# S5 channels copied unscaled from PSUM, the 1/rms applied on transposed chunks, with a new step order and a mirrored table

## The chip, the cores and the metric

The kernel runs on one core of one Trainium2 chip, in one launch. The metric is the device time of that launch in microseconds (us). TensorE (PE) multiplies matrices, VectorE (DVE) and ScalarE (ACT) work on elements, GpSimd (POOL) does so too and issues one of the two big DMA queues, SyncE (SP) issues the other. Each engine runs its own list of instructions in order and waits on semaphores for the others.

## The reference, cut to what matters

A two-layer encoder works on 512 prompt tokens and 32 sample tokens. Layer A, in which everything of this change lies:

```python
z = rms_norm(h, norm_mix_g[layer]) @ w_mix_in[layer]      # 1024 -> 768 S5 channels + 256 memory channels
mq = rms_norm(z_mem per head, mem_q_norm_g[layer])
mem_out = memory_attend(mq, mem_k[layer], mem_v[layer])   # 4 heads, 256 memory tokens
# S5: 48 groups of 16 channels, 64 complex states each
bu = einsum(z_mix per group, bb);  h_t = lam * h_{t-1} + bu_t;  y = Re(c h) + d_skip * u
y = gelu(y);  mix_out = y * sigmoid(y @ w_glu + b_glu)
h = h + concatenate([mix_out, mem_out]) @ w_mix_out[layer]
h = h + conv_ffn(rms_norm(h, norm_ffn_g[layer]))
```

Layer B has latent attention in place of S5. The rms_norm is x * rsqrt(mean(x²) + eps) * g. The gain g lies in the weights' side of the product, and 1/rms is one number for each token, so it can be multiplied on after the product with w_mix_in.

## The kernel before, in words

Activations lie with channels on the partitions and the 544 tokens along the free axis. Every big fp32 weight block is loaded raw by SP (`wraw`), rounded by ACT to a high half (`whi`, L231), reduced by ACT to what is left with its sign turned (`wlo`, L232), and completed by an accumulating DMA of POOL (L233). Three buffers of each kind are in use. A product is then three matmuls for each block and each of two column halves of 272 (`gemm`, L324). The order of instructions is worked out while the kernel is built: code that stands later is moved ahead by the priorities of the table `ORDER` (L63), which `pri` and `unit` apply, and buffers come from first-in first-out lists (`Slots`).

The input product gives eight tiles of 128 channels: six for S5 (`zts`), two for the memory attention (`zm`). `z0_end` (L963 to L976) takes each from PSUM with three (or two) DVE multiplications by `rb`, a tile in which 1/rms of every token is broadcast to all partitions (`norm_bcast`). Tokens are grouped into 69 chunks of 8 (64 of the prompt, one of zeros, 4 of the sample).

S5 is worked as six steps, one for each tile of 8 groups.
- `s5_params` (L544 to L668) builds once, on DVE, the table `tab` of the powers of lambda over chunks by doubling (levels of L646 to L649), and the powers inside a chunk `prd`.
- `s5_wv` and `s5_wvt` make the matrices that map a chunk's input to its end state. `s5_wc` (L693 to L715) makes those that map the state to the 8 outputs (three DVE operations, L698 and L700), and with matmuls (L704) the kernel taps inside a chunk; the taps `kp` are completed on POOL (L711), written to DRAM (`kd`, L714) and read back as Toeplitz blocks by 8 POOL loads (`s5_kernel`, L717 to L725).
- `s5_input` (L727 to L747) transposes a tile so that chunks lie on the 69 partitions (L733), ACT copies it out of PSUM (L735), and transposes it back in another order (L743, L744).
- `s5_scan` (L749 to L787): two matmul groups, then DVE: multiply by the table (L767 on), a running sum (L774), multiply back (L777), combine (L783, L784). It ends with `hh`, the states.
- `s5_output` (L789 to L812): L795 multiplies inputs by the Toeplitz blocks, L796 the states by `wc`, ACT copies (L800), transposes (L807), GELU (L808, L809).

The step loop (L1047 to L1073) writes, for step m: scan m, input m+1, output m-1, and at the end `do_wc(m+1)`. `mem_kv` (L335 to L406, matmuls L347, transposes L401), the keys and values of the prompt's memory tokens, is put between as a filler. After the loop come output 5, and the GLU loop (L1088 to L1099, six products by `w_glu` with L324). `mem_attend` (L417 to L523) is a generator: one piece (the norms: L427 to L452) and the first part stand ahead of the GLU loop, the others inside it at m = 1, 2, 4 and 5. `mix_out` (L814) follows.

Of the kernel before, what the change touches and what calls it, by code (L numbers as in the profile page):

```python
# [20 lines left out]
NS = 32  # L21
# [29 lines left out]
for _n, _w in (("mix", 2 * KD), ("bglu", NM), ("ffn", 2 * KD), ("kv", KD), ("mem", 2 * KD), ("ql", NM),  # L51
# [12 lines left out]
         "s5_input": 260, "norm0": 20, "s5_params": -50, "mem_attend0": 100, "s5_wc": 10, "q_front0": 10, "norm1": 0,  # L64
# [73 lines left out]
def body(ctx, tc, A, O):  # L138
# [5 lines left out]
    FW = 576  # L144
# [39 lines left out]
    warm = F.get(576)  # L184
# [3 lines left out]
    for _ in range(2):  # L188
        T.matmul(b, warm[:, 64:192], warm[:, 64:], start=True, stop=True)
# [90 lines left out]
    def norm_bcast(r, bs):  # L280
# [5 lines left out]
        rb = F.get(NT)  # L286
        V.tensor_copy(rb[:, :NP], pa)
        V.tensor_copy(rb[:, S0:], pb[:, :NS])
        bs.put(pa, pb)
        return rb  # L290
# [126 lines left out]
    def mem_attend(l, zm, kv_p, kv_s, fm, bm, out):  # L417
        ktp, vp = kv_p
        kts, vs = kv_s
# [21 lines left out]
        r = rsqrt(x, 128, 17, "zr")  # L441
        mx, nm, su, ri = (sm(17, n) for n in ("zmx", "znm", "zsu", "zri"))
# [101 lines left out]
    def s5_params(pool, tmp, sp5):  # L544
# [93 lines left out]
        V.memset(tab[:, 0, :, 0:1], 1.0)  # L638
        V.memset(tab[:, 1, :, 0:1], 0.0)
        SR = NPR * 70  # L640
        for o, lvl, c0, n in ((1, 0, 0, 1), (2, 1, 0, 2), (4, 2, 0, 4), (8, 3, 0, 8), (16, 4, 0, 16), (32, 5, 0, 16),
                              (48, 5, 16, 16), (64, 6, 0, 1)):
            t0 = view(tmp, [[NPR * n, 2], [n, NPR], [1, n]])
            t1 = view(tmp, [[NPR * n, 2], [n, NPR], [1, n]], H)
            src = view(tab, [[SR, 2], [70, NPR], [1, n]], c0)
            V.tensor_tensor(t0, src, view(sc, [[0, 2], [1, NPR], [0, n]], NPR * (lvl + 1)), ALU.mult)  # L646
            V.tensor_tensor(t1, src, view(sc, [[0, 2], [1, NPR], [0, n]], NPR * (8 + lvl + 1)), ALU.mult)
            V.tensor_tensor(tab[:, 0, :, o:o + n], t0[:, 0], t1[:, 1], ALU.subtract)
            V.tensor_tensor(tab[:, 1, :, o:o + n], t0[:, 1], t1[:, 0], ALU.add)  # L649
        V.tensor_copy(view(tab, [[70, 2 * NPR], [1, 5]], 65), view(tab, [[70, 2 * NPR], [1, 5]]))  # L650

        prd = pool.tile([128, 2, 9, 48], F32, name="prd")
        xq = pool.tile([128, 49, 16], F32, name="xq")
        P.memset(xq[:, 48], 0.0)
        for half in range(2):
            a = slice(64 * half, 64 * half + 64)
            for gh in range(2):
                c = slice(64 * gh, 64 * gh + 64)
                for i, src in enumerate((pr, pi)):
                    S.activation(view(prd[a], [[48, 9], [8, NM], [1, 4]], 432 * i + 4 * gh),  # L660
                                 view(src[c], [[NPR, 9], [4, NM], [1, 4]]), AF.Copy)
# [4 lines left out]
        P.memset(q["kp"], 0.0)  # L666
        q["hf"] = pool.tile([128, NM, 8, 2], F32, name="hf")
# [25 lines left out]
    def s5_wc(q, m, fs, fd, fb, bs):  # L693

        pk = bs.get(512)
        c, d = fd.get(8, 9, 16), fb.get(8, 9, 16)
        for o, x in ((c, 0), (d, 1)):
            V.tensor_tensor(o, view(q["cc"], [[16, 8], [0, 9], [1, 16]], 16 * (48 * x + 8 * m)),  # L698
                            view(q["prd"], [[1, 8], [48, 9], [0, 16]], 432 * x + 8 * m), ALU.mult)
# [27 lines left out]
    def s5_input(zt, fs, bs):  # L727

        zT = [fs.get(4, 8, 16, p=69) for _ in range(2)]
        for qd in range(2):  # L730
            b = bs.get(512)
            for s_ in range(4):
                T.transpose(b[:69, 128 * s_:128 * s_ + 128], view(zt, [[8, 69]], 7 - 4 * qd - s_), ident)  # L733
            for gh in range(2):
                S.activation(view(zT[gh], [[128, 4], [16, 4], [1, 16]], 64 * qd),  # L735
                             view(b[:69], [[16, 4], [128, 4], [1, 16]], 64 * gh), AF.Copy)
            bs.put(b)
        yield
        u = fs.get(8, 69)
        for gh in range(2):  # L740
            b = bs.get(512)
            for i in range(4):
                T.transpose(b[:, 69 * i:69 * i + 69], zT[gh][:, i].rearrange("p a b -> p (a b)"), ident[:69, :69])  # L743
            S.activation(u[:, 4 * gh:4 * gh + 4, :].rearrange("p a b -> p (a b)"), b[:, :276], AF.Copy)  # L744
            bs.put(b)
        fs.put(*zT)
# [42 lines left out]
    def s5_output(u, wc, kk, hh, yg, fs, bs):  # L789
        yT = [fs.get(4, 8, 16, p=69) for _ in range(2)]  # L790
        b = [bs.get(512) for _ in range(2)]
        for gh in range(2):
            for i in range(4):
                o = b[gh][:69, 128 * i:128 * i + 128]
                T.matmul(o, u[:, 4 * gh + i, :], kk[gh][:, i], start=True, stop=False)  # L795
                T.matmul(o, hh[:, 4 * gh + i, 0:69], wc[:, 4 * gh + i, 1:9].rearrange("p a b -> p (a b)"), start=False,  # L796
# [167 lines left out]
    def z0_end(m, ps, bs):  # L964
        if m < NM:
            zt = FY.get(552)
            P.memset(zt[:, 512:520], 0.0)
            V.tensor_tensor(zt[:, 0:272], ps[0][:, :272], rb[:, :272], ALU.mult)
            V.tensor_tensor(zt[:, 272:512], ps[1][:, :240], rb[:, 272:512], ALU.mult)
            V.tensor_tensor(zt[:, 520:552], ps[1][:, 240:272], rb[:, S0:], ALU.mult)  # L970
            zts.append(zt)
        else:
            z = F.get(NT)
            evac_rows(z, ps, rb)
# [18 lines left out]
    with pri("norm0"):  # L993
        rb = norm_bcast(r0, BS)
# [29 lines left out]
    wvs = []  # L1024
# [11 lines left out]
    g_in, g_out = s5_input(zts[0], F, BS), None  # L1036
# [8 lines left out]
    for m in range(NM):  # L1045
# [18 lines left out]
        if m < NM - 1:  # L1064
            do_wc(m + 1)
# [19 lines left out]
    mo = []  # L1085
# [719 lines left out]
```

## Time and profile before

| | before |
|---|---|
| median of 3 runs | 1437.56 us (1436.07 to 1439.15) |
| the profiled run | 1436.17 us |
| its span | 1434.4 us |
| busy: PE, DVE, ACT, POOL | 98%, 50%, 52%, 27% |
| last scan's last DVE operation begins | 150.33 us |
| first GLU matmul | 171.45 us |

The profile shows one execution. "Busy" is the time in which an engine has an instruction in work; matmuls are pipelined, so a busy PE is not a PE at its peak. A window is a stretch of the span. PEclk is the granted clock of TensorE as a share of its full speed. The chain of waits goes back from the last instruction, at each step to what released it. Times of instructions overlap by a little on one engine, so the spacing from one start to the next says better what one costs.

### The profile page before, as it was taken

The page shows a single profiled execution, that of the slowest core. Times are in us where ns is not written, and L with a number is a line of the kernel's source. Part 1 is how long each engine was busy: PE and PEld are TensorE (multiplying, and loading weights), DVE is VectorE, ACT ScalarE, POOL GpSimd, SP SyncE. Part 2 cuts the span into 40 slices and gives each one's busy share as a digit, 9 for nine tenths or more (in the row PEclk, how much of TensorE's full clock was granted, in tenths as well). Part 3 has the DMA queues.
Part 4 walks back from the last instruction along what each step waited for, and adds up shares of the span by engine and source line. Part 5 has one row for each costly group of instructions (what it writes and reads, how often), then busy time and mean ns, then how long its engine had stood idle before and what let it go on. Part 6 is the DMA issues. An engine that isn't in the chain of part 4 may idle for free.

```text
span 1434.4 us, 26764 instructions
## 1 busy us (share of the span) xinstructions
PE 1402.3 (98%) x10661; PEld 1299.2 (91%) x10661; DVE 714.6 (50%) x1776; ACT 740.6 (52%) x1237; POOL 385.7 (27%) x668
## 2 busy tenths in 40 slices
PE   7999899999999999999989999999999999999998
PEld 6966689999999999999978986558999999999998
DVE  7999642555315541555357545663455514551351
ACT  6556464655435543555644554654565534553452
POOL 2065333222111211133336222332322211221121
PEclk8999899999999999999999999999999999999999
DMA  9443548788788888868741521103778887888775
GB/s 268 109 118 104 151 109 190 161 173 180 171 175 175 175 175 175 176 145 196 154 118 56 158 71 45 30 1 74 170 169 176 176 177 173 176 175 177 171 157 140
DMA packets 66045, 210.59 MB, mean 147 GB/s; under 512 B 9152, under 2 KB 11424, under 8 KB 65920
## 3 DMA queue, kind: packets, MB, share of 16 engines
q0 software_dynamic: 29152, 96.61, 37.4%
q1 hardware_dynamic: 35616, 110.17, 26.6%
q10 hardware_dynamic: 1152, 2.10, 0.4%
q8 instruction: 84, 1.38, 0.4%
q14 instruction: 41, 0.34, 0.1%
HBM read 203.22 MB, written 5.61 MB: 146 GB/s over the span
## 4 chain that ended last, share of the span: by engine, by line
PE 87%; DMA 4%; DVE 3%; ACT 2%; issue 2%; POOL 1%; SPq 0%; ACTq 0%; DVEq 0%; POOLq 0%
PE bank L324 67%; PE bank L1312 2%; PE bank L1560 2%; PE bank L1399 2%; PE bank L1596 1%; DMA wlo<-i_w_in 1%; PE bank L1513 1%; PE bank L1487 1%; PE bank L1585 1%; PE bank L347 1%; DMA wlo<-i_w_f 1%; PE bank L1201 1%; PE bank L479 1%; PE bank L1427 1%; PE bank L517 1%
## 5 line engine op out<-in xcount | busy, mean ns | idle before, releaser
L324 PE MATMUL bank<-rc,whi 128*128 128x272 f32 x3728 | 625.3, 289 | 0.2 <-DVE rc L305 0.2
L324 PEld LDWEIGHTS bank<-rc,whi 128*128 128x128 f32 x3728 | 528.2, 188 | 4.2 <-issue 3.1
L324 PE MATMUL bank<-rc,wlo 128*128 128x272 f32 x1864 | 388.3, 288 | 0.5 <-DMA wlo<-i_w_in 0.3
L231 ACT ACTIVATE whi<-wraw 128x1024 fp32r<-128x1024 f32 (+2 forms) x178 | 182.9, 1028 | 354.3 <-issue 304.0
L324 PEld LDWEIGHTS bank<-rc,wlo 128*128 128x128 f32 x1864 | 293.2, 188 | 1.3 <-DMA wlo<-i_w_in 0.5
L324 PE MATMUL bank<-g,whi 128*128 128x272 f32 x1408 | 234.8, 288 | 0.8 <-ACT g L216 0.8
L324 PEld LDWEIGHTS bank<-g,whi 128*128 128x128 f32 x1408 | 198.9, 188 | 1.4 <-ACT g L216 1.2
L233 POOL DMA_DIRECT2D wlo<-i_w_f x136 | 116.7, 858 | 303.9 <-ACT wlo L232 302.5
L232 ACT ACTIVATE wlo<-wraw 128x1024 fp32r<-128x1024 f32 (+2 forms) x178 | 180.6, 1015 | 0.6 <-PE bank L1513 0.5
L324 PE MATMUL bank<-g,wlo 128*128 128x272 f32 x704 | 145.6, 288 | 2.1 <-DMA wlo<-i_w_f 2.1
L855 DVE SCALAR_TENSOR_TENSOR fa<-fa,gp,fa 128x546 f32<-128x546 f32 x88 | 69.6, 791 | 139.6 <-ACT fa L854 139.6
L869 DVE TENSOR_TENSOR h<-bank,h 128x272 f32<-128x272 f32 x96 | 38.2, 435 | 173.2 <-PE bank L324 172.6
L324 PEld LDWEIGHTS bank<-g,wlo 128*128 128x128 f32 x704 | 110.3, 188 | 2.5 <-DMA wlo<-i_w_f 2.5
L854 ACT ACTIVATE fa<-fa,gp 128x546 f32<-128x546 f32 x88 | 73.1, 831 | 12.5 <-DVE fa L849 12.5
L847 DVE TENSOR_TENSOR fa<-bank,fa 128x272 f32<-128x272 f32 x88 | 38.9, 442 | 80.5 <-PE bank L324 76.7
L856 DVE SCALAR_TENSOR_TENSOR fa<-fa,gp,fa 128x546 f32<-128x546 f32 x88 | 69.5, 790 | 3.1
L895 ACT ACTIVATE fa<-fa 128x546 f32<-128x546 f32 x44 | 29.1, 662 | 71.7 <-DVE fa L856 71.7
L851 POOL COPY fa<-gp 128x2 f32<-128x2 f32 x88 | 19.9, 227 | 170.2 <-DVE g L217 107.9
L852 POOL COPY fa<-fa 128x4 f32<-128x4 f32 x88 | 18.2, 207 | 164.5 <-DVE fa L849 164.5
L324 PE MATMUL bank<-ra,whi 128*128 128x272 f32 x256 | 47.7, 309 | 2.7 <-ACT whi L241 2.7
L216 ACT ACTIVATE g<-fa 128x544 fp32r<-128x544 f32 x44 | 28.9, 658 | 37.6 <-DVE fa L897 37.6
L896 DVE TENSOR_TENSOR fa<-fa,fa 128x512 f32<-128x512 f32 x44 | 30.5, 693 | 33.5 <-ACT fa L895 33.5
(628 smaller groups left out, 1987.2 us busy)
## 6 DMA issues: line engine op xcount, KB each, us to landing
wraw<-i_w_f SPq DMA_DIRECT2D x120, 512.0 KB, 4.9
wlo<-i_w_f POOLq DMA_DIRECT2D x120, 512.0 KB, 7.4
wraw<-i_w_out SPq DMA_DIRECT2D x16, 512.0 KB, 4.4
wlo<-i_w_out POOLq DMA_DIRECT2D x16, 512.0 KB, 7.0
wraw<-i_w_in SPq DMA_DIRECT2D x14, 512.0 KB, 5.1
wlo<-i_w_in POOLq DMA_DIRECT2D x14, 512.0 KB, 7.5
wraw<-i_w_f SPq DMA_DIRECT2D x16, 384.0 KB, 3.1
wlo<-i_w_f POOLq DMA_DIRECT2D x16, 384.0 KB, 5.9
```

The costliest lines, as they stand in the source:

```text
L216: S.activation(hi, src, AF.Copy)
L231: S.activation(hi, raw, AF.Copy)
L232: S.activation(lo, raw, AF.Copy, scale=-1.0)
L233: P.dma_start(lo, ap, accum_op=ALU.add)
L324: T.matmul(ps[q][:, :c], ww, xx[:, c0:c0 + c], start=k == 0 and i == 0, stop=k == n - 1 and i == 2)
L847: V.tensor_tensor(u[:, 2:274], ps[0][:, :272], rb[:, :272], ALU.mult)
L854: S.activation(y, u[:, 2:548], AF.Identity, scale=gcol("cw", 3 * ci + 2), bias=gcol("cb", ci))
L855: V.scalar_tensor_tensor(y, u[:, 1:547], gcol("cw", 3 * ci + 1), y, ALU.mult, ALU.add)
L856: V.scalar_tensor_tensor(y, u[:, 0:546], gcol("cw", 3 * ci), y, ALU.mult, ALU.add)
L869: V.tensor_tensor(h[m][:, c0:c0 + cc], ps[qd][:, :cc], h[m][:, c0:c0 + cc], ALU.add)
L895: S.activation(yg, yg, AF.Silu)
L896: V.tensor_tensor(u[:, 2:514], ya[:, :NP], yg[:, :NP], ALU.mult)
```

## The change

The S5 stage is changed in four ways.

First, the six S5 tiles are copied from PSUM by ACT without 1/rms. `rb` gets a gap of 8 zeros between prompt and sample so that it has the same 69 chunks of 8, and 8 PE transposes and 2 ACT copies make from it `sr`, 69 chunks by 8 positions. In `s5_input`, where chunks are on the partitions, ACT's copies multiply by a column of `sr`; there are 8 copies of 128 elements per partition and step in place of 4 of 256. The copies go to one tile (`FZ`, a part of the memory in which the table's scratch lay).

Second, the table is centred: column 32 holds power 0, and columns 0 to 31 are the mirror of columns 33 to 64 with the imaginary part's sign turned, copied by ACT. Two levels of the doubling go.

Third, the powers inside a chunk go from 9 to 8, `wc` from 1152 to 1024 elements, the matmul of the taps is split into 16 and 112 columns, and the D-skip term is made once.

Fourth, the order: `do_wc(m+1)` stands ahead of input m+1, not at the end of step m; the norms of the memory attention are a unit at m = 3, and its other pieces stand at m = 1 to 5 of the GLU loop, with a new priority. A few buffer counts and widths follow.

```diff
-         "s5_input": 260, "norm0": 20, "s5_params": -50, "mem_attend0": 100, "s5_wc": 10, "q_front0": 10, "norm1": 0,
+         "s5_input": 260, "norm0": 20, "s5_params": -50, "mem_attend0": 30, "s5_wc": 10, "q_front0": 10, "norm1": 0,
...
-        for o, lvl, c0, n in ((1, 0, 0, 1), (2, 1, 0, 2), (4, 2, 0, 4), (8, 3, 0, 8), (16, 4, 0, 16), (32, 5, 0, 16),
-                              (48, 5, 16, 16), (64, 6, 0, 1)):
+        for o, lvl, c0, n in ((1, 0, 0, 1), (2, 1, 0, 2), (4, 2, 0, 4), (8, 3, 0, 8), (16, 4, 0, 16), (32, 5, 0, 1)):
...
-        V.tensor_copy(view(tab, [[70, 2 * NPR], [1, 5]], 65), view(tab, [[70, 2 * NPR], [1, 5]]))
+        for i, s in ((0, 1.0), (1, -1.0)):
+            S.activation(tab[:, i, :, 0:32], view(tab, [[70, NPR], [-1, 32]], SR * i + 64), AF.Copy, scale=s)
+        S.activation(view(tab, [[70, 2 * NPR], [1, 5]], 65), view(tab, [[70, 2 * NPR], [1, 5]], 32), AF.Copy)
...
-        c, d = fd.get(8, 9, 16), fb.get(8, 9, 16)
+        c, d = fd.get(8, 8, 16), fb.get(8, 8, 16)
...
-                T.matmul(pk[32 * i:32 * i + 32, 128 * gh:128 * gh + 128],
-                         view(q["xq"], [[1, 32]], 16 * (8 * m + 4 * gh + i)),
-                         c[:, 4 * gh + i, 0:8].rearrange("p a b -> p (a b)"), start=True, stop=True)
+                T.matmul(o[:, :16], x, q["cc"][:, 0, 8 * m + g], start=True, stop=True)
+                T.matmul(o[:, 16:], x, c[:, g, 0:7].rearrange("p a b -> p (a b)"), start=True, stop=True)
...
-            for gh in range(2):
-                S.activation(view(zT[gh], [[128, 4], [16, 4], [1, 16]], 64 * qd),
-                             view(b[:69], [[16, 4], [128, 4], [1, 16]], 64 * gh), AF.Copy)
+            for s_ in range(4):
+                s = 7 - 4 * qd - s_
+                S.activation(view(zT, [[128, 8], [1, 16]], 64 * qd + 16 * s_), view(b[:69], [[16, 8], [1, 16]], 128 * s_),
+                             AF.Copy, scale=sr[:, s:s + 1])
...
-            V.tensor_tensor(zt[:, 0:272], ps[0][:, :272], rb[:, :272], ALU.mult)
-            V.tensor_tensor(zt[:, 272:512], ps[1][:, :240], rb[:, 272:512], ALU.mult)
-            V.tensor_tensor(zt[:, 520:552], ps[1][:, 240:272], rb[:, S0:], ALU.mult)
+            S.activation(zt[:, 0:272], ps[0][:, :272], AF.Copy)
+            S.activation(zt[:, 272:512], ps[1][:, :240], AF.Copy)
+            S.activation(zt[:, 520:552], ps[1][:, 240:272], AF.Copy)
...
+        for qd in range(2):
+            b = BS.get(512)
+            for s_ in range(4):
+                T.transpose(b[:69, 128 * s_:128 * s_ + 128], view(rb, [[8, 69]], 4 * qd + s_), ident)
+            S.activation(sr[:, 4 * qd:4 * qd + 4], view(b[:69], [[128, 4]]), AF.Copy)
+            BS.put(b)
...
         if m < NM - 1:
-            g_in = s5_input(zts[m + 1], F, BS)
+            do_wc(m + 1)
+            g_in = s5_input(zts[m + 1], sr, F, FZ, BS)
...
-        if m < NM - 1:
-            do_wc(m + 1)
+        if m == 3:
+            unit("att_norms", att)
...
-    att = mem_attend(0, zm, kvp, kvs, F, BS, mo)
-    unit("mem_attend0", att)
     BS.merge(BG)
     for m in range(NM):
-        if m in (1, 2, 4, 5):
+        if m:
             unit("mem_attend0", att)
```

The built order shows the move on three engines. From the first matmul of `mix_out` on, all engines have the same instructions in the same order in both kernels.

On DVE, around the last scans: L698 and L700 are `do_wc` of the last step (`wc_868`), L777 to L784 a scan's end, L767 the start of the next scan. Before:

```order
L674 TENSOR_TENSOR tb_865<-bs_396,pi_398 128x1024
L777 TENSOR_TENSOR fa_91<-fa_77,tab 128x560
L777 TENSOR_TENSOR fa_86<-fa_77,tab 128x560
L676 TENSOR_TENSOR wv_864<-wv_864,tb_865 128x1024
L783 TENSOR_TENSOR big<-fa_91,fa_86 64x280
L784 TENSOR_TENSOR big<-fa_91,fa_86 64x280
...
L698 TENSOR_TENSOR wc_868<-cc_399,prd 128x1152
L698 TENSOR_TENSOR tb_865<-cc_399,prd 128x1152
L217 TENSOR_TENSOR rc_1767<-fa_80,rc_1766 128x544
L700 TENSOR_TENSOR wc_868<-wc_868,tb_865 128x1152
L767 TENSOR_TENSOR fa_74<-bank_63,tab 128x4x69
```

And after, where L702 and L704 are the same `do_wc` (`wc_878`), L778 to L788 a scan's end and L771 a scan's start:

```order
L778 SCALAR_TENSOR_TENSOR fa_71<-fa_74,fa_75 128x560
L680 TENSOR_TENSOR wv_873<-wv_873,tb_875 128x1024
L781 TENSOR_TENSOR fa_77<-fa_71,tab 128x560
L781 TENSOR_TENSOR fx_868<-fa_71,tab 128x560
L702 TENSOR_TENSOR wc_878<-cc_411,prd 128x1024
L787 TENSOR_TENSOR fx_872<-fa_77,fx_868 64x280
L788 TENSOR_TENSOR fx_872<-fa_77,fx_868 64x280
...
L702 TENSOR_TENSOR tb_875<-cc_411,prd 128x1024
L431 COPY fx_868<-fa_87 64x32 x2
L704 TENSOR_TENSOR wc_878<-wc_878,tb_875 128x1024
L771 TENSOR_TENSOR fx_869<-bank_63,tab 128x4x69
```

Before, the last `wc` stands between the scans of steps 4 and 5; after, between those of steps 3 and 4.

On PE, from the last output product of the stage to the GLU: before, with L795 and L796 the end of output 5, L427 to L479 memory attention, L324 the first GLU matmul:

```order
L795 MATMUL bank_63<-fa_72,fa_75 69x128
L796 MATMUL bank_63<-wc_868,fa_78 69x128
L401 MATMUL bank_68<-cn,fx_860 128x128 x4
L807 MATMUL bank_69<-cn,fa_86 128x69 x4
L807 MATMUL bank_70<-cn,big 128x69 x4
L427 MATMUL bank_68<-cn,fa_71 128x2 x4
L479 MATMUL bank_66<-fa_89,fa_87 128x256
L479 MATMUL bank_67<-fa_89,fa_87 128x256
L427 MATMUL bank_68<-cn,fa_74 128x2 x4
L436 MATMUL bank_68<-cn,fa_76 128x1 x2
L446 MATMUL bank_69<-fa_79,fa_73 128x256 x2
...
L324 MATMUL bank_68<-rc_1766,whi_98 128x272
```

And after, from the same place (L799 and L800 end output 5, L811 are its transposes, L324 is the GLU):

```order
L799 MATMUL bank_68<-fa_76,fa_74 69x128
L800 MATMUL bank_68<-wc_878,fa_72 69x128
L324 MATMUL bank_67<-rc_1874,whi_96 128x272
L324 MATMUL bank_67<-rc_1875,whi_96 128x272
L811 MATMUL bank_70<-cn,fx_872 128x69
L401 MATMUL bank_69<-cn,fa_92 128x128 x4
L811 MATMUL bank_70<-cn,fx_872 128x69 x3
L811 MATMUL bank_63<-cn,fx_871 128x69 x4
L324 MATMUL bank_67<-rc_1874,wlo_99 128x272
L324 MATMUL bank_67<-rc_1876,whi_96 128x272
```

GLU matmuls now begin right behind output 5 and between its transposes; the attention's norms and products no longer stand ahead of them.

On ACT, at the start, where L231 and L232 make the weight halves of a tile of the input product (`whi_96` is the fourth tile's) and L560 prepares S5's parameters. Before:

```order
L231 ACTIVATE whi_98<-wraw_95 128x1024
L232 ACTIVATE wlo_101<-wraw_95 128x1024
L559 ACTIVATE cc_399<-cc_399 64x768
L560 ACTIVATE cc_399<-cc_399 128x768
L231 ACTIVATE whi_96<-wraw_93 128x1024
L232 ACTIVATE wlo_99<-wraw_93 128x1024
```

And after, with L972 to L974 the copies of the first two S5 tiles out of PSUM:

```order
L231 ACTIVATE whi_98<-wraw_95 128x1024
L232 ACTIVATE wlo_101<-wraw_95 128x1024
L560 ACTIVATE cc_411<-cc_411 64x768
L972 ACTIVATE fa_80<-bank_64 128x272
L973 ACTIVATE fa_80<-bank_65 128x240
L974 ACTIVATE fa_80<-bank_65 128x32
L972 ACTIVATE fa_81<-bank_66 128x272
L973 ACTIVATE fa_81<-bank_67 128x240
L974 ACTIVATE fa_81<-bank_67 128x32
L561 ACTIVATE cc_411<-cc_411 128x768
L231 ACTIVATE whi_96<-wraw_93 128x1024
L232 ACTIVATE wlo_99<-wraw_93 128x1024
```

Six copies that depend on PE's products now stand ahead of the fourth tile's weight halves.

## Rows read from the trace of the kernel before

**Rows 1.** The page, part 1: busy us (share of the span) xinstructions.

```profile
PE 1402.3 (98%) x10661; PEld 1299.2 (91%) x10661; DVE 714.6 (50%) x1776; ACT 740.6 (52%) x1237; POOL 385.7 (27%) x668
```

**Rows 2.** Windows: stretch, us, PE PEld DVE ACT POOL busy, PEclk, DMA share, GB/s.

```profile
33.00:69.00 36.00, 36.00 (x287) 35.62 (x287) 34.27 (x83) 17.20 (x37) 2.71 (x5) 1.00 0.55 120
70.00:150.00 80.00, 75.19 (x664) 52.01 (x662) 76.49 (x124) 41.66 (x107) 46.55 (x78) 0.98 0.41 118
150.00:160.00 10.00, 5.61 (x27) 4.69 (x28) 6.04 (x23) 5.91 (x16) 7.95 (x13) 0.61 0.66 136
```

**Rows 3.** Chain of waits, S5 stage: start us, us, what was on it.

```profile
96.85 0.57 PE bank L704 x16
97.42 1.05 PE bank L347 x2
98.48 0.50 PE bank L733 x4
...
100.34 0.22 PE bank L795 x2
...
126.94 1.28 DVE wc L700
...
144.18 6.59 DMA kd<-kp
...
151.66 4.71 DMA fa<-kd
...
156.41 0.69 PE bank L795 x2
...
163.18 0.22 PE bank L795 x2
...
165.81 1.05 PE bank L427 x8
...
171.45 2.83 PE bank L324 x16
```

**Rows 4.** Timeline, DVE: start us, us, instruction; first scan's start, last scan's end.

```profile
71.52 0.45 DVE L767 TENSOR_TENSOR fa<-bank,tab 128x276 f32<-128x276 f32 x1 [0.66 <-PE bank L756]
...
150.33 0.45 DVE L784 TENSOR_TENSOR fa<-fa,fx 64x280 f32<-64x280 f32 x1
```

**Rows 5.** Timeline, DVE, 54 to 58.5 us.

```profile
54.48 0.95 DVE L647 TENSOR_TENSOR big<-tab,p_sc 128x768 f32<-128x768 f32 x1
55.35 1.35 DVE L698 TENSOR_TENSOR wc<-cc,prd 128x1152 f32<-128x1152 f32 x1
56.62 0.55 DVE L648 TENSOR_TENSOR tab<-big 128x384 f32<-128x384 f32 x1
57.09 0.55 DVE L649 TENSOR_TENSOR tab<-big 128x384 f32<-128x384 f32 x1
57.56 0.43 DVE L968 TENSOR_TENSOR fa<-bank,fa 128x272 f32<-128x272 f32 x1
57.91 0.95 DVE L646 TENSOR_TENSOR big<-tab,p_sc 128x768 f32<-128x768 f32 x1
```

**Rows 6.** Groups on ACT, 69 to 215 us: count, busy us, mean ns, idle before.

```profile
L735 ACT ACTIVATE fa<-bank 69x256 f32<-69x256 f32 x10 | 3.6, 377 | 4.1 <-POOL kp L711 2.9 <-PE bank L733 1.2
...
L809 ACT ACTIVATE fa<-bank 128x16 f32<-128x16 f32 x12 | 3.0, 248 | 0.0
```

**Rows 7.** Timeline, ACT, 20 to 37 us: in brackets the idle time before.

```profile
19.82 0.85 ACT L560 ACTIVATE cc<-cc 128x768 f32<-128x768 f32 x1
...
22.28 1.04 ACT L232 ACTIVATE wlo<-wraw 128x1024 fp32r<-128x1024 f32 x1
...
36.13 1.06 ACT L231 ACTIVATE whi<-wraw 128x1024 fp32r<-128x1024 f32 x1 [5.46 <-PE bank L324]
```

**Rows 8.** Timeline, PE, 21 to 24 us.

```profile
22.91 0.28 PE L260 MATMUL bank<-cn,fa 128*128 128x1 f32 x2
```

More of the change, by code (lines that the diff above doesn't have):

```diff
@@ L183, in body @@
     h = [base.tile([128, NT], F32, name=f"h{k}") for k in range(KD)]
-    warm = F.get(576)
+    warm = F.get(560)
     V.memset(warm, 0.0)
@@ L188, in body @@
     for _ in range(2):
-        T.matmul(b, warm[:, 64:192], warm[:, 64:], start=True, stop=True)
+        T.matmul(b, warm[:, :128], warm[:, :512], start=True, stop=True)
     B.put(b)
@@ L285, in norm_bcast @@
         T.transpose(pb[:, :NS], r[:NS, 4:5].to_broadcast([NS, 128]), ident[:NS, :NS])
-        rb = F.get(NT)
+        rb = F.get(so + NS)
         V.tensor_copy(rb[:, :NP], pa)
-        V.tensor_copy(rb[:, S0:], pb[:, :NS])
+        V.tensor_copy(rb[:, so:], pb[:, :NS])
         bs.put(pa, pb)
@@ L414, in mem_cache, with mem_attend @@
         return kt, v
-    def mem_attend(l, zm, kv_p, kv_s, fm, bm, out):
-        ktp, vp = kv_p
-        kts, vs = kv_s
+    def mem_attend(l, zm, kv_p, kv_s, fm, bm, out, early=False):
         ps = bm.get(512)
@@ L441, in mem_attend @@
         r = rsqrt(x, 128, 17, "zr")
+        if early:
+            yield
+        (ktp, vp), (kts, vs) = kv_p, kv_s() if early else kv_s
         mx, nm, su, ri = (sm(17, n) for n in ("zmx", "znm", "zsu", "zri"))
@@ L666, in s5_params @@
         P.memset(q["kp"], 0.0)
+        q["dd"] = pool.tile([128, 2 * NM, 16], F32, name="dd")
+        P.tensor_tensor(q["dd"], view(cn, [[0, 2 * NM], [1, 16]], 128), view(q["dsk"], [[1, 2 * NM], [0, 16]]), ALU.mult)
         q["hf"] = pool.tile([128, NM, 8, 2], F32, name="hf")
@@ L725, in s5_kernel, with s5_input @@
         return kk
-    def s5_input(zt, fs, bs):
-        zT = [fs.get(4, 8, 16, p=69) for _ in range(2)]
+    def s5_input(zt, sr, fs, fz, bs):
+        zT = fz.get(8, 8, 16, p=69)
         for qd in range(2):
@@ L795, in s5_output @@
                 T.matmul(o, u[:, 4 * gh + i, :], kk[gh][:, i], start=True, stop=False)
-                T.matmul(o, hh[:, 4 * gh + i, 0:69], wc[:, 4 * gh + i, 1:9].rearrange("p a b -> p (a b)"), start=False,
+                T.matmul(o, hh[:, 4 * gh + i, 0:69], wc[:, 4 * gh + i].rearrange("p a b -> p (a b)"), start=False,
                          stop=True)
@@ L973, in z0_end @@
             z = F.get(NT)
-            evac_rows(z, ps, rb)
+            V.tensor_tensor(z[:, 0:272], ps[0][:, :272], rb[:, :272], ALU.mult)
+            V.tensor_tensor(z[:, 272:512], ps[1][:, :240], rb[:, 272:512], ALU.mult)
+            V.tensor_tensor(z[:, S0:], ps[1][:, 240:272], rb[:, 520:552], ALU.mult)
             zm.append(z)
@@ L993, in body @@
     with pri("norm0"):
-        rb = norm_bcast(r0, BS)
+        rb = norm_bcast(r0, BS, 520)
+        P.memset(rb[:, 512:520], 0.0)
+        sr = lp.tile([69, 8], F32, name="sr")
+        for qd in range(2):
[4 more added lines that the diff above has]
+            BS.put(b)
     for m in range(3):
@@ L1007, in body @@
     lr = exr.enter_context(tc.tile_pool(name="l0b", bufs=1, reuse_waits="tile"))
-    R, fx = slots(lr, 2, F32, 512, "rb"), slots(lr, 3, F32, FW, "fx")
-    FA, FB, FD = slots(lr, 2, F32, 1024, "wv"), slots(lr, 1, F32, 2 * FW, "tb"), slots(lr, 3, F32, 2 * FW, "wc")
+    fx = slots(lr, 5, F32, FW, "fx")
+    FA, FB, FD = slots(lr, 2, F32, 1024, "wv"), slots(lr, 1, F32, 1024, "tb"), slots(lr, 3, F32, 1024, "wc")
     fxs = list(fx.free)
     F.merge(fx)
-    F.merge(Slots([big[:, FW * i:FW * i + FW] for i in range(4)]))
+    F.merge(Slots([big[:, FW * i:FW * i + FW] for i in range(2)]))
+    FZ = Slots([big[:, 2 * FW:]])
     kvp = F.get(2, NMEM), F.get(2, 256)
-    mkv = mem_kv(F, R, BG, BS, (kvp, (mk1, mv1)))
+    mkv = mem_kv(F, F, BG, BS, (kvp, (mk1, mv1)))
     fills = ((1, 2, 1), (1, 1, 0), (1, 0, 0), (0, 1, 0), (1, 1, 0), (1, 1, 0), (7,))
@@ L1023, in fill @@
             nfill += 1
-    wvs = []
+    wvs, mo = [], []
+    att = mem_attend(0, zm, kvp, lambda: kvs, F, BS, mo, True)
     def products(m):
```

38 lines of the change are left out of this document (18 added, 20 removed).

## The prediction

> **What bounds the kernel now.** I read the page's totals first. PE is busy 1402.3 us of 1434.4 and no other engine over 52% [rows 1], so a change on DVE, ACT or POOL can only pay where PE waits or runs slowly. Since the built order is the same in both kernels from the first `mix_out` matmul on, that place must lie ahead of it, in the S5 stage.
>
> Next the windows [rows 2]. From 33 to 69 us PE has no gap: the input product runs. DVE is full there too, 34.27 of 36. From 70 to 150, the six scans, PE is busy 75.19 of 80 and DVE 76.49 of 80: two engines that are both nearly full, and DVE the fuller. ACT has 41.66 and POOL 46.55. From 150 to 160 PE is busy 5.61 of 10, at a clock of 0.61.
>
> Then the chain of waits, to see which of the two sets the end [rows 3]. Behind the fifth scan it goes over DVE's `wc` (L700, 126.94), to the write of the last taps to DRAM (144.18, 6.59 us until it landed), the loads that bring them back (151.66, 4.71) and only then to output 5 (L795, 156.41). The last scan itself was over at 150.33 + 0.45 = 150.78 [rows 4]. So there are two things to gain: scans that end sooner, and a round trip through DRAM that ended 5.6 us behind the last scan.
>
> **DVE's part.** The spacing of starts [rows 5] gives the cost of each form: 768 elements 55.35 - 54.48 = 0.87; 1152 elements 56.62 - 55.35 = 1.27; 384 elements 57.09 - 56.62 = 0.47; a 272-column evacuation 57.91 - 57.56 = 0.35. Between the 768 and the 1152, 1024 elements come to about 1.13; in proportion to the 272, 240 columns cost 0.31 and 32 about 0.1.
> - Evacuations: 6 tiles x (0.35 + 0.31 + 0.1) = 4.6 us leave DVE.
> - Table: two levels of 16, each 2 x 0.87 + 2 x 0.47 = 2.68, so 5.35, and a copy of five columns, 0.2.
> - `wc`: 18 operations, each shorter by 1.27 - 1.13 = 0.14, 2.5 us.
>
> Together 12.7 us of an engine that is 0.95 busy from 33 to 150. What is saved ahead of 69 us isn't lost, since DVE takes up `wv` and `wc` of later steps there.
>
> **PE's part.** Added are 8 transposes for `sr`; four of the same kind took 0.50 (L733) [rows 3], so 1.0 us. The split of the taps' matmul adds 48 matmuls. Sixteen passes of L704 took 0.57 [rows 3], 0.036 each, for 8 matmuls, so a matmul is two passes and there are 96 more. The columns remain the same, so the least is nothing and the most 96 x 0.036 = 3.4; I take 1.5, near the middle, since a pass of 16 columns has an eighth of the work. PE therefore gets 1.0 to 4.4 us more, 2.5 taken.
>
> [...]
>
> **ACT's and POOL's part.** ACT gets 18 evacuations and, per step, 8 copies of 128 elements for 4 of 256. A copy of 256 took 377 ns, one of 16 took 248 [rows 6], so one of 128 about 0.31: 2.5 for 1.5, or 1.0 us more per step, 5 over the five in the window, beside 41.66 busy of 80. The two mirrors are some 0.85 each, as the 768 elements of L560 [rows 7]. I cost all of it at nothing in the scans, since ACT has half of its time free; if that cover went, it would be 1.0 us for each of the six steps. ACT's copies for `zT` must also wait for the table, whose scratch they overwrite. The table now ends some 5 us sooner, so I count no wait. On POOL six small operations become one; nothing waits for it.
>
> **When the last scan ends.** If DVE alone were the bound, it would come sooner by 12.7 less the transposes in its way, 1.0: 11.7. If PE alone were, it could take up only its idle time from 70 to 150, 80 - 75.19 = 4.8 [rows 2], and would pay the 2.5: 2.3. In the trace DVE has the smaller gap, 3.5 against 4.8, but these are so near that PE must become the bound after a few us. I take 5, nearer to PE's end, and keep 2.3 to 11.7.
>
> **From the last scan to `mix_out`.** Three things end late in the kernel before.
> - The round trip. With `do_wc` one step earlier (on DVE between the scans of steps 3 and 4, not 4 and 5) the taps are read back about 12 us sooner, a scan's length, from (150.78 - 71.52) / 6 = 13.2 [rows 4]. They were 156.41 - 150.78 = 5.6 late [rows 3, 4], so they are now early, and output 5 waits only for its scan: -5.6.
> - Output 5 ran at the low clock behind that wait. Its 8 pairs of matmuls and the two L347 groups between took from 156.41 to 163.18, 6.77; at the paces seen around 100 us they take 8 x 0.22 + 2 x 1.05 = 3.86 [rows 3]. With no gap of 4.4 us [rows 2] ahead, I count -2.9. [...]
> - The attention's norms and first products stood alone between output 5 and the GLU, 165.81 to 171.45, 5.6 us [rows 3]. Their matmuls are still to be done, beside the GLU's. Only the waits among them go, 2.5 of it by estimate, since they are short matmuls with ACT and DVE in between.
>
> That is -11.0. Against it, the 5.6 us were cover for the way from output 5 to the GLU (ACT's copy, transposes, GELU, two splits), some 4 us, of which the GLU's first matmuls, now moved between these transposes, hide a part: +3. So -8. The ends are -11, with all of it hidden, and -5, if the round trip alone goes.
>
> **Sum.** -5 - 8 = -13: 1436.17 - 13 = 1423.2 for the profiled run. The median of the runs lies 1.4 over that run, so 1424.6. The ends are -2.3 - 5 = -7 and -11.7 - 11 = -23.
>
> **The rivals.**
>
> A, the forecast: -13, with a range of its own of -17 to -9, 1420.5 to 1428.5.
>
> B, the relief of DVE is eaten by the next wait, and only the round trip pays. In the scans PE is at 94% [rows 2] and works in order, so that what DVE saves comes back as waits for POOL, whose memset for a scan stands behind eight loads of taps in its list, or for a `wc` buffer that an output must free first. For it: two engines are nearly full at once. Against it: PE has 4.8 us of idle time, and the order on DVE has some slack at each scan's start. Price: -6 (0 to -1 in the scans, -5 to -6 behind them), 1431.5.
>
> C, DVE is the bound throughout, as its smaller gap says, and PE has more slack than "busy" shows, since busy holds waits inside pipelined matmuls. Then the scans give their -11.7 and the tail -8: -20, 1417.9. Against it: PE's 2.5 us of new work, and fillers that are placed by count and not by time.
>
> D, slower. Weight halves queue behind evacuations on ACT. Before, the fourth tile's `wlo` was done at 22.28 + 1.04 = 23.3 [rows 7]. After, two tiles' copies stand ahead of it in the list and wait for PE's products, which go on past 22.9 [rows 8]; then 1.0 for three copies, 0.75 for the copy of `cc` and 2 x 0.95 to 1.04 for the halves, which ends near 26.4: 3.1 late. If every one of tiles 3 to 7 lost that, 15.5 us, it would be +2.5 on top of A's gain and +9.5 on top of B's, 1440 to 1447, 1443 taken. It decides from 13 / 5 = 2.6 us per tile on. Against it: further on, ACT stood idle for 5.46 us ahead of a tile's L231, waiting for PE to free the buffers [rows 7], and it was busy only 17.20 of 36 [rows 2]; so one late tile can happen, five can't easily. I count nothing for it in A.
>
> That the change would do nothing (within 0.2%, 2.9 us, which is about what a measurement of this kernel can tell from no change) needs B and part of D together.
>
> **How the numbers follow.** A 0.57, B 0.20, C 0.14, D 0.07, and 0.02 for what I have not seen. The time is A's, 1424.6. The range goes from beyond C's middle, 1413, so that it holds most of C with A's outer tail, to 1434, which holds most of B: left out are D and about a tenth of the others. Faster by over 0.2%: A and C 0.71, and three quarters of B 0.15, so 0.86. Within it: the rest of B and half of the unseen, 0.06. Slower: D and the other half, 0.08.
>
> **What would show it.** In the changed kernel's profile: the last scan's last DVE operation near 145 to 147 in place of 150.33; L799 of output 5 with no wait for a load of taps; a window behind the last scan with PEclk near 1.0; the first GLU matmul directly behind output 5, near 155; `mix_out` 12 to 14 us sooner, and the same span behind it. B would show DVE with gaps between 70 and 140 and the last scan at 150. C would show DVE still full and PE without new waits. D would show PE waiting for `wlo<-i_w_in` between 33 and 69, where it has no gap now. The forecast is wrong if the scans' end moves by under 2 us, or if the GLU's matmuls wait for splits or for attention pieces by more than the 3 us counted.

## The result and the profile after

The changed kernel took 1447.81 us (median of 4 runs, 1444.84 to 1448.44) beside 1438.19 of the kernel before: 1.0065 of it, 95% interval 1.0046 to 1.0084. It is slower by 0.65%; 1424.6 and faster had been forecast.

Windows of the profile after, the columns as in [rows 2]:

```profile
33.00:69.00 36.00, 36.00 (x292) 35.74 (x292) 31.52 (x64) 19.66 (x51) 2.78 (x4) 1.00 0.54 123
70.00:150.00 80.00, 77.44 (x792) 56.22 (x790) 71.81 (x132) 50.94 (x136) 42.09 (x80) 1.00 0.43 123
150.00:160.00 10.00, 7.46 (x45) 5.52 (x46) 7.78 (x28) 7.21 (x20) 4.05 (x6) 0.96 0.48 156
160.00:170.00 10.00, 6.93 (x32) 6.26 (x31) 3.76 (x12) 3.73 (x9) 1.32 (x3) 0.52 0.55 149
```

DVE lost work where it should (31.52 from 34.27 and 71.81 from 76.49), ACT gained it, and from 150 to 160 the clock is 0.96 in place of 0.61. But the low clock has only moved: it held from 152.3 to 162.5 us before and holds from 159.3 to 169.5 after (0.50 in both stretches), now under the first GLU matmuls. The last window holds a new gap; a second one lies between 230 and 240 us. The timelines show where the chain stands at four points; first the last scan's end on DVE, then three places on PE:

```profile
150.57 0.45 DVE L788 TENSOR_TENSOR fa<-fa,fa 64x280 f32<-64x280 f32 x1
```

```profile
157.85 0.49 PE L324 MATMUL bank<-rc,whi 128*128 128x272 f32 x2 [1.88 <-DVE fa L390]
...
163.68 0.60 PE L324 MATMUL bank<-rc,wlo 128*128 128x272 f32 x1 [3.07 <-DMA wlo<-i_w_glu]
...
233.91 0.52 PE L324 MATMUL bank<-rc,wlo 128*128 128x272 f32 x2 [4.31 <-DMA wlo<-i_w_out]
```

The last scan ends when it did [rows 4]. The first GLU matmul comes at 157.85, against 171.45 [rows 3] 13.6 us sooner, as much as the whole gain that was forecast. All of it and 12 us more is lost behind that. The first addition of `mix_out` to `h` on DVE marks it, of the kernel after and of the one before:

```profile
229.02 0.79 DVE L827 TENSOR_TENSOR h<-bank,h 128x272 f32<-128x272 f32 x2 [1.90 <-PE bank L324]
```

```profile
221.88 0.79 DVE L823 TENSOR_TENSOR h<-bank,h 128x272 f32<-128x272 f32 x2 [2.28 <-PE bank L324]
```

From the first GLU matmul to here are 71.2 us after and 50.4 before: 20.8 us lost. Behind it the kernel after has 1446.6 - 229.0 = 1217.6 us left and the one before 1434.4 - 221.9 = 1212.5: 5.1 more, for the wait of 4.31 at 233.91 and the low clock (0.50) from 234.4 to 237.8. The sum, -13.6 + 20.8 + 5.1 = 12.3, is the difference of the spans, 12.2.

A part of the 20.8 is work that stood ahead of the GLU before. So it is clearer to count from the end of the last scan, which lies within 0.3 us in both traces: to the first addition it is 78.0 us after and 71.1 before, 6.9 more. GLU matmuls take 5.2 us more there (some at the low clock of 0.50) and PE is idle for 1.6 us more; output 5 takes 3.8 less, the attention's norms, 2.4 us, now run among the scans, and smaller groups take 0.6 less. What remains is the memory attention's scores, value products and transposes. Counted from each start to the next start on PE, without idle time, they take 19.9 us after and 13.1 before, 6.8 more: scores 2.9, value products 4.1, transposes 0.3 less.

The rows tell why. Each of these matmuls stands in the trace as two passes. A score uses 64 of the array's 128 rows (64*128), a value product 64 of its columns (128*64), and in the code two heads use different halves. Before:

```profile
166.79 0.70 PE L479 MATMUL bank<-fa,fa 64*128 64x256 f32 x4
...
180.77 1.13 PE L479 MATMUL bank<-fa,fa 64*128 64x256 f32 x4
...
189.20 1.94 PE L517 MATMUL bank<-fa,fa 128*64 128x512 f32 x8
191.07 2.65 PE L479 MATMUL bank<-fa,fa 64*128 64x256 f32 x16
```

and after:

```profile
181.38 0.70 PE L480 MATMUL bank<-fa,fa 64*128 64x256 f32 x4
...
192.44 1.07 PE L518 MATMUL bank<-fa,fa 128*64 128x512 f32 x2
...
202.25 0.70 PE L480 MATMUL bank<-fa,fa 64*128 64x256 f32 x2
202.88 0.39 PE L324 MATMUL bank<-rc,wlo 128*128 128x272 f32 x1
```

Four passes at 166.79 or at 181.38 take as long, 0.70 us, as the two at 202.25. In the built order the four are two neighbours on different halves, and their single records start two at a time, 7 ns apart: they run in pairs. The four at 180.77 are two neighbours on the same half; their records start one by one, 0.22 us apart, and take 1.13. So one pass costs 0.22 us alone and a pair costs the same here (in the row at 191.07 pairs start at 191.39, 191.60 and 191.82). On top of that every run between other matmuls pays about 0.2 us (an estimate from 0.63 us for two single passes and 1.06 for four, start to next start), so that short runs are dear as well. For value products, eight passes in pairs take 1.94 and two alone 1.07. The pairs of all the passes, and their time from start to start:

| kernel | scores: pairs of 16 possible, us | values: pairs of 8 possible, us |
|---|---|---|
| before | 10, 6.5 | 8, 3.7 |
| after | 2, 9.4 | 0, 7.9 |
| before with the attention's new place (b_att_new) | 6, 8.2 | 0, 7.9 |
| after with priority 100 (a_pri100) | 2, 7.6 | 8, 3.7 |
| after with the attention's old place (a_att_old) | 8, 8.1 (part at the low clock) | 8, 3.7 |
| before with the score loops exchanged (b_samehalf) | 4, 8.1 (part at the low clock) | 8, 3.7 |

### The profile page after: what moved, and what is told of

Read it like the earlier page. It is cut to its first block, busy times and chain, and to the rows that moved or that the text cites. A ratio compares the mean times of both kernels' runs of the same rounds, so it can differ in the third digit from the quotient of the medians.

```text
span 1446.6 us, 26990 instructions
## 1 busy us (share of the span) xinstructions
PE 1411.7 (98%) x10765; PEld 1302.7 (90%) x10765; DVE 708.1 (49%) x1751; ACT 752.6 (52%) x1284; POOL 376.3 (26%) x664
## 3 DMA queue, kind: packets, MB, share of 16 engines
q10 hardware_dynamic: 1152, 2.10, 0.4%
## 4 chain that ended last, share of the span: by engine, by line
PE 86%; DMA 4%; issue 4%; ACT 2%; DVE 2%; POOL 2%; SPq 0%; DVEq 0%; POOLq 0%; ACTq 0%
PE bank L324 66%; PE bank L1327 2%; PE bank L1575 2%; PE bank L1414 2%; PE bank L1611 1%; PE bank L480 1%; DMA wlo<-i_w_f 1%; PE bank L1528 1%; PE bank L1502 1%; PE bank L1600 1%; PE bank L347 1%; PE bank L1216 1%; PE bank L518 1%; PE bank L1442 1%; DMA wlo<-i_w_out 1%
## 5 line engine op out<-in xcount | busy, mean ns | idle before, releaser
L324 PE MATMUL bank<-rc,whi 128*128 128x272 f32 x3728 | 630.2, 290 | 2.1 <-DVE fa L390 1.9
L324 PEld LDWEIGHTS bank<-rc,whi 128*128 128x128 f32 x3728 | 530.7, 189 | 9.6 <-issue 6.2
L324 PE MATMUL bank<-rc,wlo 128*128 128x272 f32 x1864 | 390.7, 290 | 7.4 <-DMA wlo<-i_w_out 4.3
L231 ACT ACTIVATE whi<-wraw 128x1024 fp32r<-128x1024 f32 (+2 forms) x178 | 182.9, 1027 | 359.7 <-issue 316.3
L324 PEld LDWEIGHTS bank<-rc,wlo 128*128 128x128 f32 x1864 | 294.6, 189 | 10.2 <-DMA wlo<-i_w_out 4.5
L324 PE MATMUL bank<-g,whi 128*128 128x272 f32 x1408 | 233.8, 288 | 0.8 <-ACT g L216 0.8
L324 PEld LDWEIGHTS bank<-g,whi 128*128 128x128 f32 x1408 | 198.3, 188 | 1.4 <-ACT g L216 1.2
L232 ACT ACTIVATE wlo<-wraw 128x1024 fp32r<-128x1024 f32 (+2 forms) x178 | 180.5, 1014 | 0.6 <-PE bank L1528 0.5
L324 PE MATMUL bank<-g,wlo 128*128 128x272 f32 x704 | 145.7, 288 | 1.9 <-DMA wlo<-i_w_f 1.9
L324 PEld LDWEIGHTS bank<-g,wlo 128*128 128x128 f32 x704 | 110.2, 188 | 2.6 <-DMA wlo<-i_w_f 2.6
L324 PE MATMUL bank<-ra,whi 128*128 128x272 f32 x256 | 47.2, 307 | 2.2 <-ACT whi L241 2.2
```

The source lines that it names most:

```text
L231: S.activation(hi, raw, AF.Copy)
L232: S.activation(lo, raw, AF.Copy, scale=-1.0)
L324: T.matmul(ps[q][:, :c], ww, xx[:, c0:c0 + c], start=k == 0 and i == 0, stop=k == n - 1 and i == 2)
```

## The experiments

Ratios are to the kernel before, run beside each. The theory: the attention's new place and priority cost the time (P). Its rival: the S5 edits do (S). Each edit is shown as changed from the kernel it starts from.

**The attention's old place in the changed kernel.**

```diff
-"mem_attend0": 30
+"mem_attend0": 100
-        if m == 3:
-            unit("att_norms", att)
+    att = mem_attend(0, zm, kvp, kvs, F, BS, mo)
+    unit("mem_attend0", att)
-        if m:
+        if m in (1, 2, 4, 5):
```

> The changed kernel with the memory attention's old place and priority (norms and sample part ahead of the GLU, the other pieces at m = 1, 2, 4, 5, priority 100); all else as changed. Theory P (the new place of the attention costs the time: its score and value matmuls run in pairs on two halves of TensorE's array when they stand side by side, and singly when GLU matmuls stand between them, and the GLU gets longer so that weights come late): 1424 to 1432 us, score matmuls x4 in about 0.6 us again, no wait of 4 us for w_out's low halves. Theory S (the S5 edits cost it: the scans did not end sooner, ScalarE is fuller, and the attention only shows it): 1442 us or more.

Measured 0.9953 (0.9928 to 0.9978), 1434.62 us beside 1441.88: 1.1% faster than the changed kernel by the ratios. The value products run in pairs again, of the scores 8 pairs of before's 10 are back, and from 215 to 245 us PE has no gap. P holds: 0.9953 of the first comparison's 1438.19 is 1431.4, inside its range.

**The attention's new place alone, in the kernel before** (the same lines the other way, with the early stop in `mem_attend` that they need).

> The kernel before with nothing but the attention's new place and priority (norms at m = 3, pieces at m = 1 to 5, priority 30). Theory P: slower than before by 8 to 18 us, 1446 to 1456, with single score matmuls of about 0.31 us each and a wait for w_out's low half. Theory S: 1430 to 1438, since the attention's norms no longer stand alone ahead of the GLU.

1.0091 (1.0064 to 1.0117), +13 us. In its trace no value product is paired, PE waits 4.8 us for `w_out`'s low half, and scores, values and transposes take 18.4 us in place of 13.1. P holds from this side too, and S falls: the S5 edits are not needed for the loss.

**The priority alone.**

```diff
-"mem_attend0": 30
+"mem_attend0": 100
```

> The changed kernel with the attention's priority back from 30 to 100, its new place kept. In the built order most score matmuls then stand in runs of two and four and the value matmuls in fours. Theory P: most of the loss goes, 1428 to 1438 us. Theory S, or if the place and not the mixing costs it: 1444 to 1449.

0.9949 (0.9929 to 0.9969): one number is worth 1.2%. The wait for `w_out` is nearly gone:

```profile
221.31 0.52 PE L324 MATMUL bank<-rc,wlo 128*128 128x272 f32 x2 [0.44 <-DMA wlo<-i_w_out]
```

Scores, values and transposes take 14.9 us, 4.9 less than with 30: all value pairs are back, and the scores stand in fewer runs. Here the mixing costs and not the place, since with the old place the ratio is the same (0.9953). With `do_wc` at the end of the step it is otherwise, as the table of corners below shows.

**Must the two halves alternate?** The kernel before, with the score loops exchanged:

```diff
-                for t in range(2):
-                    for i in range(2):
+                for i in range(2):
+                    for t in range(2):
```

> The kernel before with the two inner loops of the score matmuls exchanged: the same matmuls side by side, but two of the same array half follow each other, then two of the other. Theory P in its strict form (only neighbours on different halves run together): 32 passes of which half lose their partner, +2.5 to +5 us, and 16 score passes in about 4 to 5 us in place of 2.65. If what costs is the mixing with GLU matmuls of another shape, and not the missing neighbour: no change, within 1 us.

1.0029 (1.0011 to 1.0047), about 4 us slower by the ratio, as the strict form expected; 1.7 us of it are the scores. The rows bear that form out in the main:

```profile
177.19 1.13 PE L479 MATMUL bank<-fa,fa 64*128 64x256 f32 x4
...
194.26 2.10 PE L479 MATMUL bank<-fa,fa 64*128 64x256 f32 x8
...
204.46 1.99 PE L479 MATMUL bank<-fa,fa 64*128 64x256 f32 x12
```

The first four passes, 0.70 us before, take 1.13 now that they are on one half, and eight in a row with no GLU matmul between them take 2.10, all single. So standing side by side is not enough. Nor is the alternation strictly needed: of the twelve at 204.46 the first eight ran in four pairs, though the list has two matmuls of one half and then two of the other. In all, 4 pairs are left of 10. What decides when a later matmul of the other half is taken along is open. Neighbours on different halves can miss each other too: after, at 189.11, the second value product began at 189.97, behind its copy out of PSUM (DVE's L511, 189.22 and 0.69 long), and the four passes ran singly, in 1.93 us.

**do_wc early alone, in the kernel before.**

```diff
         if m < NM - 1:
+            do_wc(m + 1)
             g_in = s5_input(zts[m + 1], F, BS)
-        if m < NM - 1:
-            do_wc(m + 1)
```

> The kernel before with nothing but do_wc(m+1) moved ahead of input m+1. The prediction's term (the round trip of the last taps and output 5 at the low clock, 5.6 + 2.9 us, go): 0.993 to 0.996 of before, no wait for taps ahead of output 5. Rival (the loads of taps then stand ahead of a scan's memset and of weights in POOL's list, and TensorE is the bound of the scans anyway): 0.998 to 1.003, with a scan that waits for POOL.

1.0055 (1.0031 to 1.0079), slower by 8 us, outside both ranges; the rival's mechanism is there. Output 5 doesn't wait for taps any more, but the third scan ends at 113.25 in place of 107.11 and the last at 156.96 in place of 150.33 (starts of the last operation). From 90 to 110 us PE stands idle for 5.0 of 20, against 0.6 before, and the clock is 0.66 against 0.91. POOL's, ACT's and PE's rows say on what (in brackets idle time and releaser):

```profile
93.08 1.76 POOL L723 DMA_DIRECT2D big<-kd  x3
94.83 1.11 POOL L711 TENSOR_TENSOR kp<-kp,fa 128x32 f32<-128x32 f32 x1
```

```profile
95.97 0.60 ACT L687 ACTIVATE fa<-bank 128x512 f32<-128x512 f32 x1 [1.82 <-POOL kp L711]
```

```profile
96.91 0.49 PE L756 MATMUL bank<-fa,big 128*64 128x69 f32 x2 [2.54 <-ACT fa L744]
```

Loads of taps, some 0.6 us each to issue, stand in POOL's list ahead of L711. ACT's L687 waits for that, ACT's L744 stands behind L687, and the next scan's matmuls (L756) wait for L744.

**do_wc at its old place in the changed kernel, with the attention's old place and with its new one.**

```diff
-            do_wc(m + 1)
             g_in = s5_input(zts[m + 1], sr, F, FZ, BS)
+        if m < NM - 1:
+            do_wc(m + 1)
```

> The changed kernel with the memory attention's old place (as in a_att_old, which took 0.9953 of before) and also with do_wc back at the end of the step. What is left of the change is the arithmetic: copies on ScalarE, mirrored table, eight powers, split matmul. Theory R (only the earlier round trip of the taps through DRAM paid, the 12.7 us less work on DVE did not, since TensorE bounds the scans): 0.999 to 1.002 of before, output 5 waits for its taps again. Theory A (the arithmetic paid): 0.993 to 0.996, as a_att_old.

> The changed kernel with nothing but do_wc back at the end of the step (new place and priority of the attention kept). It fills the fourth corner beside the change (1.0065), a_att_old (0.9953) and a_att_wc_old (0.9918). If the early do_wc costs what b_wc_early showed (+0.55%): 1.000 to 1.004. If it costs nothing in the changed kernel and the attention's place is all: 1.005 to 1.008.

With the attention's old place 0.9918 (0.9902 to 0.9935), 1429.74 us, the lowest ratio of all, though output 5 waits 1.30 us for its taps again. Theory R's range is excluded; that it is the arithmetic which paid is not shown, since the split of the taps' matmul alone comes to 0.9936 (below) and the ranges overlap. With the new place 1.0106 (1.007 to 1.0142). The corners, with a third row from the runs with priority 100:

| | do_wc early | do_wc at the end |
|---|---|---|
| attention new, priority 30 | 1.0065 (the change) | 1.0106 |
| attention new, priority 100 | 0.9949 | 0.9988 |
| attention old, priority 100 | 0.9953 | 0.9918 |

Place and priority of the attention together make 1.1 and 1.9%, in the two columns. The place alone (the last two rows) makes nothing with `do_wc` early and 0.7% with `do_wc` at the end. The effect of `do_wc` is smaller, 0.35 to 0.4%, and has no constant sign, so neither of my two expectations for a_wc_old holds.

**Who bounds the scans?** a_att_old with the six tiles copied by DVE:

```diff
-            S.activation(zt[:, 0:272], ps[0][:, :272], AF.Copy)
+            V.tensor_copy(zt[:, 0:272], ps[0][:, :272])
```

(and so for the two other pieces).

> a_att_old with the unscaled copies of the six S5 tiles done by VectorE in place of ScalarE: 4.6 us of DVE work put back. If TensorE bounds the scans: as a_att_old, 0.994 to 0.9965. If DVE does: 3 to 4.6 us more, 0.9975 to 0.9985.

0.9961 (0.9946 to 0.9976), as a_att_old: 4.6 us of DVE work change nothing that can be measured in the whole. In the trace the last scan's last operation begins 2.0 us later (152.83 against 150.84), so a part of it may still count in the scans.

**The split of the taps' matmul alone, and its control.** The kernel before with `c[:, 4 * gh + i, 0]` and `1:8` in two matmuls; and, without any split, with `tc.cur_priority += 1` behind each of the 48.

> The kernel before with nothing but the taps' matmul split into 16 and 112 columns: 96 passes more. If TensorE bounds the scans: +2 to +3.5 us at 0.02 to 0.036 us each, 1.0014 to 1.0025. If DVE bounds them: within 0.7 us.

> The kernel before with no instruction more or less: the counter from which the priorities are taken is raised by one behind each of the taps' 48 matmuls, as 48 more instructions would raise it, so that other instructions swap places. b_wcsplit, with 48 more matmuls, was faster by 0.64%. If the reshuffled order does that and not the split: a change of the order of 0.3% or more, either way. If order is worth little: 0.998 to 1.002.

The split kernel took 0.9936 (0.9919 to 0.9953), faster by 9 us where a loss or no change was expected, and the control 1.0001 (0.9983 to 1.0019). But the control did not reshuffle what it was to reshuffle. In its trace DVE, ACT and POOL have exactly the order of the kernel before, and in the built order PE's list differs in 14 places; in the split kernel the order differs from before in 24 places on DVE, 26 on ACT and 13 on POOL. So a reshuffled order is not excluded as the cause of the split's gain. Nor does the split, which adds work to PE alone, fit a TensorE that bounds the scans. In the split kernel's trace output 5 begins at 154.26 and does not wait for taps, and its GLU begins at 166.78; why is open.

**The low half of the GLU's first weights by DVE**, from a_pri100 (for the loop's first product alone):

```diff
-            S.activation(lo, raw, AF.Copy, scale=-1.0)
-            P.dma_start(lo, ap, accum_op=ALU.add)
+            lo_eng.tensor_tensor(lo, raw, hi.bitcast(F32), ALU.subtract)
```

> a_pri100 (0.9949 of before) with the low half of the first GLU weights made by one VectorE subtraction, not by ScalarE and an accumulating DMA. In the changed kernel the GLU's third matmul waits until 163.7 us for that DMA. Theory W (weights that come late hold the GLU once it starts early): the wait goes, -3 to -5 us, 0.991 to 0.993. Rival (the last S5 output's split, ready at 163.5, holds it anyway): 0.994 to 0.996.

0.9959 (0.9944 to 0.9974), as a_pri100. But this does not speak for the rival, for the edit missed the wait. DVE's row and PE's:

```profile
140.37 0.95 DVE L236 TENSOR_TENSOR wlo<-wraw,whi 128x768 fp32r<-128x768 f32 x1
```

```profile
162.71 0.60 PE L327 MATMUL bank<-rc,wlo 128*128 128x272 f32 x1 [3.98 <-DMA wlo<-i_w_glu]
```

DVE made its low half more than 20 us early, and PE still waits 3.98 us for a DMA. In the built order the matmul at 162.71 reads the weights of the loop's second product, which are still completed by POOL's DMA (the one at 163.68 in the changed kernel reads the same). Whether the GLU gains when that low half comes sooner was not tested.

**Two attempts at more.** a_att_wc_old with priority 160, and the changed kernel with priority 100 and `do_wc` at the end:

> a_att_wc_old (0.9918 of before: the arithmetic of the change, with the old places of the attention and of do_wc) with the attention's priority 160 in place of 100; in the built order all its score matmuls then stand in runs of four and eight and the value matmuls in fours. If the pairing of neighbours is worth what b_samehalf and the rows say: 1 to 3 us less, 0.990 to 0.9915. If not: 0.9915 to 0.994.

> The changed kernel with do_wc back at the end of the step and the attention's priority back at 100, its new place kept: what the runs so far point to as the mildest repair. If both costs add up: 0.989 to 0.993 of before. If the new place itself costs (weights of the GLU come late): 0.994 to 0.997.

0.9954 (0.9933 to 0.9974) and 0.9988 (0.9976 to 1.0): misses, the costs don't add up. In the second one's trace the values run in pairs and no score does; in the first one's only half of the value pairs are left, so more priority is not simply better. A second trace of the kernel before:

> The kernel before, unchanged, once more, for a second trace of it: the one at hand is among its fastest executions (1436.17, against medians of 1440 and 1442 beside the other runs). If the later start of weights in the input product makes the difference between executions: waits for w_in's low halves of over 4 us between 20 and 69 us. If it is the tail: output 5 later than 156.4 us by as much as the whole is longer.

Its span is 1435.5, 1.1 more than the first; it has waits of 3.9 us for `w_in`'s low halves and of 2.7 for taps. It was too near the first trace to decide between the two.

## Why the prediction was wrong

**The step that failed** is the third of the tail: "Their matmuls are still to be done, beside the GLU's. Only the waits among them go, 2.5 of it by estimate". I took a matmul to cost the same wherever it stands. It didn't: mixed with the GLU's, the attention's scores and value products lost their pairs and cost 7.0 us more (6.8 with the transposes). And the GLU, started before its weights were there and stretched to 71.2 us, met waits of 3.07 and, at its end, 4.31 us for low halves of weights, the first within the low clock from 159.3 to 169.5, the second ahead of another 3.4 us of it. In the table place and priority together are worth a loss of 1.1 to 1.9%, 16 to 27 us, where 2.5 of gain were counted; a_pri100 shows that with `do_wc` early the priority, which sets the mixing, is all of it. Lost pairs and shorter runs account for about 7 of these us; the rest is waits and clock, whose shares no run separates. The price could have been read in the trace before: 1.13 us for four passes without pairs and 0.70 in pairs. And the built order, in which GLU matmuls stand between the attention's all through the GLU, was read only for where the GLU begins. No rival named it.

**The scans' end.** -5 was counted, and the last scan's last operation moved from 150.33 to 150.57. DVE's relief is real, 2.8 and 4.7 us in the two windows, and in the trace the second scan ended 4.7 us sooner (88.16 against 92.86, starts of the last operation); the third took it all back (108.04 against 107.11). Rival B had it so for the scans (0 to -1, gaps on DVE, the last scan at 150), and an end that moves by under 2 us was the prediction's own sign of being wrong. It is less even than the 2.3 that I gave for PE alone. PE was busy 77.44 of 80, and its new work (the attention's norms, which I had not counted there, are 2.5 us of it) took what was free. That PE is the bound there fits a_evac_dve, but it is argued: the one edit of PE's own work, the split, came out faster.

**The round trip.** The wait went, and the clock from 150 to 160 rose from 0.61 to 0.96, both as forecast. But the low clock came back under the GLU, as long as before (10.2 us at 0.50), so the 2.9 counted for it were not gained in the whole. And in the kernel before, the earlier `do_wc` alone costs 8 us, through loads of taps in POOL's list (in the changed kernel its effect has no constant sign). The prediction named POOL's queue as a rival's reason and priced it at nothing in the forecast.

**The split.** In the trace after, 32 passes of a step lie between these two rows:

```profile
99.56 0.26 PE L710 MATMUL bank<-cc,xq 128*32 128x16 f32 x7
...
100.25 0.44 PE L799 MATMUL bank<-fx,fx 128*69 128x128 f32 x2
```

100.25 - 99.56 = 0.69 us for 32 passes, against 0.57 for 16: 0.12 more a step, about 0.7 in all by this one step, less than the 1.5 taken. This is 22 ns a pass, where the 16 before had 36 each. The passes use 32 columns each (128*32) and lie, by the code, in four column groups. The trace before showed already that such passes don't run one by one: the single records of L704 start four at a time, 7 ns apart, and 0.11 us lie from the start of one four to that of the next.

**What held.** That ACT's copies are free fits a_evac_dve: which engine makes them changes nothing in the whole. Rival D did not come: PE is busy 36.00 of 36 from 33 to 69. GLU's start was forecast near 155 and came at 157.85.

**What stays open:** why the split alone is faster by 0.64%, and with it how much of a_att_wc_old's 0.8% belongs to the arithmetic; why the attention's new place costs 0.7% with `do_wc` at the end and nothing with `do_wc` early; what late GLU weights cost; and when a matmul that is not the next neighbour is taken along as a partner.

## What to carry to other kernels

A matmul that fills half the array had a price here that depended on its neighbours (0.70 us for four passes in pairs, 1.13 for four without): before pieces are spread between full-size ones, look up in the order whether partners on the other half are torn apart, and take both prices from the trace. Use starts to next starts for that; a mean over a run mixes pairs with single passes. Before a run is read as a test, look in its trace whether the edit changed what it was meant to change. Work that moves out of a wait must have its weights and its bank there sooner as well; ask of a stage that will start early what it then waits for. A cheaper engine pays only where it is the bound; here, with PE at 94% and DVE at 96 from 70 to 150 us, the scans' end stayed (150.33 before, 150.57 after).

## What the runs showed that was not expected

- One priority number (30 or 100) was worth 1.2% of the whole kernel, while a shift of priorities on 48 places hardly changed the order and was worth nothing (1.0001).
- Two matmuls on different halves of the array ran at the same time (records that start 7 ns apart, four passes in 0.70 us against 1.13 on the same half), and eight passes of scores in a row gave no pair where they stood two and two on one half (2.10 us).
- Issuing a load of 64 KB on POOL took about 0.6 us (3 in 1.76 above, and 7 in 4.14 from 99.07 in the same trace), so that eight of them are, by estimate from that, a delay of 5 us for whatever stands behind.
- Two stretches of the trace after had a granted clock of 0.50: from 159.3 to 169.5 us, behind a wait of 1.88 us and around one of 3.07, and from 234.4 to 237.8, right behind one of 4.31.
